# ScalarE puts the residual into PSUM ahead of the down product, and six pairs of row tiles go in seven products

## Chip, cores and metric

One core of a Trainium2 chip runs the whole layer in one launch. The metric is the device time of one execution in microseconds. The engines are TensorE (PE in the profile, its weight loads PEld), VectorE (DVE), ScalarE (ACT), GpSimd (POOL) and SyncE (SP, whose queue issues all loads and stores of the stage studied here).

## What is computed

A decoder layer on x of 256 tokens by 2048: a normalised input goes through one combined projection into gated linear attention and a sparse attention, both are joined by an output projection onto the residual, and a SwiGLU follows. The change is in the last two lines:

```python
h = x + jnp.concatenate([gla_out, nsa_out], axis=-1) @ w_out
m = rms_norm(h, ffn_norm_g)
return h + (jax.nn.silu(m @ w_gate) * (m @ w_up)) @ w_down
```

w_gate and w_up are 2048 x 5632, w_down is 5632 x 2048, all float32.

## The kernel before

**Precision.** Each float32 operand is split into a high and a low part (`in_parts`, lines 563 to 565: ScalarE copies the high part, VectorE subtracts to get the low one). A product is three matmuls: high x high, high x low weights, low x high.

**The feed-forward stage** walks over the 5632 columns in 11 blocks of 512 (`FB`, `NFB`). For each block f it runs `gate_up(f)`, and then, from the second block on, `down(f - 1)`: so the down product of a block comes after the gate and up products of the next, and the last down product stands alone at the end (lines 1075 to 1082).

**gate_up** (949 to 1026). The 16 row tiles of 128 are taken as 8 pairs. A pair's weights (two tiles of gate, two of up, 512 columns each) come in by two DMAs (`load4`, three buffers "fraw"). Gate and up, both token tiles (256 tokens are two tiles of 128) and both row tiles make a 2 x 2 x 2 product: eight products of 128x128 by 128x512, each of three matmuls. Some pairs (`PAIRS7`: 0, 2, 4, 5, 6; in the first block `FIRST7`: 0, 2, 4) are done in seven products instead, by combinations of the operands as in Strassen's scheme. On the side of the activations the combinations are made once (`pair_forms`, called from `turn_h` during the output projection); on the side of the weights they are made anew for each pair and block: VectorE adds (lines 983 to 985: one TT of 1024 elements, two of 512), and the four results are split as well. So a pair in eight costs one split of 2048 elements per partition, a pair in seven one of 1536 and two of 1024, and three TTs. Split weights lie in four buffers "ftwo" (`two_parts`); a pair in seven takes two of them, one with the plain weights (used by products 1, 2, 3: nine matmuls) and one with the combinations (products 5, 7, 6, 4: twelve). `ORDER0` and `ORDER` give the order of the pairs.

**Banks.** PSUM has eight banks of 128x512 float32. The products are added up in up to eight of them, numbered 1 to 8 in the code: 1, 5, 6, 7 belong to the sevens alone, 8 to the eights alone, 2, 3, 4 to both. `bank()` hands out the next of a pool of eight, in turn. After the last seven of a block (`last7`) banks 1, 5, 6, 7 are combined: ScalarE copies bank 1 to q1 (1008), VectorE makes u, q5u, q7u, q57u (1009 to 1012). At the end of the block these are added to banks 2, 3, 4, 8, and gate and up are put together with a Silu (1020 to 1025).

**turn_act** (1030 to 1039) is a generator that is fed in between the matmuls: it transposes the block's activations on TensorE, four transposes for each token tile, into a bank, and splits them into `hi` and `lo`. It runs near the end of the next block's gate_up (`urgent`); for the last block it is fed in during the down product before.

**down** (1041 to 1057) goes over the four column quarters n of the output: one load and split of w_down, 24 matmuls for both token tiles, then VectorE adds the two banks to the residual `h_sb[n]` in SBUF (line 1055); in the last call the result is stored by SP (1057), in halves of 256 columns.

**Order of the work.** The program is written as straight Python; a scheduler then fixes the order of the instructions on each engine, and each engine works its list through in order. Semaphores for data and for buffers are set by the framework.

Of the kernel before, what the change touches and what calls it, by code (L numbers as in the profile page):

```python
# [22 lines left out]
NFB = DFF // FB  # L23
# [13 lines left out]
def kernel(  # L37
# [4 lines left out]
    nc = tc.nc  # L42
    act, mm = nc.scalar.activation, nc.tensor.matmul
# [35 lines left out]
    urgent, later = [], []  # L79
# [11 lines left out]
    def drain(queue):  # L91
        while queue:
            for _ in queue.pop(0):
                pass

    def drive(mains, pace):

        credit = 0.0
        for m in mains:
            for units in m:  # L100
                credit += units
                while credit >= pace:
                    side()
                    credit -= pace

    last = {}
# [60 lines left out]
    for c in range(2):  # L167
        k = slice(2 * c, 2 * c + 2)
# [80 lines left out]
        rsqrt_(out, ms)  # L249


    def chunk(banks, xh, xl, ws, first_, end, parts=((0, 512),), t_first=False):

        order = [(k, t) for k in range(4) for t in range(NT)]
        if t_first:
            order.sort(key=lambda kt: kt[1])
        for k, t in order:
            wh, wl = ws[k]
            for i, (a, m) in enumerate(((xh, wh), (xh, wl), (xl, wh))):
                for (off, w), bk in zip(parts, banks):  # L260
                    last["mm"] = mm(  # L261
                        bk[t], a[:, k, t * P:(t + 1) * P], m[:, off:off + w],
                        start=(first_ and k == 0 and i == 0), stop=(end and k == 3 and i == 2))
                yield 2

    n_h, n_l = [], []
# [595 lines left out]

    PAIRS7, FIRST7 = (0, 2, 4, 5, 6), (0, 2, 4)


    OLD = (1, 3)
    ORDER0, ORDER = OLD + (0, 5, 2, 4, 6, 7), (0, 1, 2, 4, 3, 5, 6, 7)
    forms = {}  # L870
    turned = set()

# [67 lines left out]
    def parts_of(src):  # L940

        if not fw:
            return split(src, 4, 512)
        n = src.shape[1]
        hi, lo = two_parts()
        in_parts(hi[:, :n], lo[:, :n], src)
        return [(hi[:, k], lo[:, k]) for k in range(n)]

    def gate_up(fb, aTs, before):

        hi, lo = g4([4, S], F32R), g4([4, S], F32R)
        aTs.append((hi, lo))
        banks = {}

        def product(q, a, w, k):

            if q not in banks:
                banks[q] = bank()
                new = True
            else:  # L960
                new = False
            for i, (x, m) in enumerate(((a[0], w[k][0]), (a[0], w[k][1]), (a[1], w[k][0]))):
                todo[q] -= 1
                mm(banks[q], x, m, start=new and i == 0, stop=todo[q] == 0)  # L964

        def tokens(k, t):
            assert k in turned
            return tuple(x[k // 4][:, k % 4, t * P:(t + 1) * P] for x in (hT_h, hT_l))

        order, sevens = (ORDER0, FIRST7) if fb == 0 else (ORDER, PAIRS7)  # L970
        last7 = max(sevens, key=order.index)
        todo = dict.fromkeys((1, 5, 6, 7), 3 * len(sevens))
        todo.update(dict.fromkeys((2, 3, 4), 3 * len(sevens) + 6 * (8 - len(sevens))))
        todo[8] = 6 * (8 - len(sevens))
        for at, pair in enumerate(order):
            if fb == 0 and at == len(OLD):
                ffn_pools()
            a, b = 2 * pair, 2 * pair + 1
            r = load4([(m[0], a, 2, fb * FB) for m in (w_gate, w_up)])
            if pair in sevens:  # L980
                w = parts_of(r[:, 0:3])
                s1, s2 = g4([2, 512]), g4([2, 512])
                TT(s1, r[:, 1:3], r[:, 3:4].to_broadcast([P, 2, 512]), ALU.add)  # L983
                TT(s2[:, 0], s1[:, 1], r[:, 1], ALU.add)  # L984
                TT(s2[:, 1], s2[:, 0], r[:, 0], ALU.add)  # L985
                f = [tuple(forms[pair][:, i, j] for i in range(2)) for j in range(4)]
                product(1, tokens(b, 0), w, 1)
                yield 2
                product(2, tokens(a, 0), w, 0)
                yield 2  # L990
                product(3, f[3], w, 2)
                yield 2
                hi_, lo_ = two_parts()
                in_parts(hi_[:, 0:2], lo_[:, 0:2], s1)
                in_parts(hi_[:, 2:4], lo_[:, 2:4], s2)
                w = [(hi_[:, k], lo_[:, k]) for k in range(4)]
                for q, x, k in ((5, f[0], 0), (7, f[2], 1), (6, f[1], 2), (4, tokens(a, 1), 3)):
                    product(q, x, w, k)
                    yield 2
            else:  # L1000
                w = parts_of(r)
                for q, t, m in ((2, 0, 0), (3, 0, 1), (4, 1, 0), (8, 1, 1)):
                    for j in range(2):
                        product(q, tokens(a + j, t), w, 2 * m + j)
                        yield 2
            if pair == last7:
                q1, u, q5u, q7u, q57u = (g2([512]) for _ in range(5))
                act(q1, banks[1], AF.Copy)
                TT(u, banks[6], q1, ALU.add)
                TT(q5u, banks[5], u, ALU.subtract)  # L1010
                TT(q7u, banks[7], u, ALU.add)
                TT(q57u, banks[5], q7u, ALU.subtract)
                if before is not None:
                    urgent.append(before)
        if fb == 0:
            drain(urgent)
            rms(rf, ssh)
            TT(rf, rf, hback, ALU.mult)
        gs = []
        for t, (g, gq, u_, uq) in enumerate(((q1, 2, q5u, 3), (q7u, 4, q57u, 8))):  # L1020
            TT(g, banks[gq], g, ALU.add)
            act(g, g, AF.Silu, scale=rf[:, t:t + 1])
# [3 lines left out]
        turns[fb] = turn_act(gs, hi, lo)  # L1026

    turns = {}

    def turn_act(gs, hi, lo):  # L1030
        for t in range(NT):
            ts = slice(t * P, (t + 1) * P)
            p = bank()
            for j in range(4):
                transpose(p[:, j * P:(j + 1) * P], gs[t][:, j * P:(j + 1) * P])
                if j % 2:
                    yield
            pv = p.rearrange("p (j s) -> p j s", j=4)
            in_parts(hi[:, :, ts], lo[:, :, ts], pv)

    def down(f0, aTs, last):

        for m in range(2):
            banks = [[bank() for _ in range(NT)] for _ in range(2)]
            for f, (ah, al) in enumerate(aTs):
                end = f == len(aTs) - 1
                for i, n in enumerate((2 * m, 2 * m + 1)):
                    ws = parts_of(load4([(w_down[0], 4 * (f0 + f), 4, n * 512)]))
                    yield from chunk([banks[i]], ah, al, ws, f == 0, end, t_first=last and end)
                    if not end:  # L1050
                        continue
                    for t in range(NT):
                        for c in range(0, 512, 256 if last else 512):
                            cs = slice(c, c + (256 if last else 512))
                            TT(h_sb[n][:, t, cs], banks[i][t][:, cs], h_sb[n][:, t, cs], ALU.add)  # L1055
                            if last:
                                nc.sync.dma_start(out[t * P:(t + 1) * P, n * 512 + c:n * 512 + c + 256], h_sb[n][:, t, cs])


    drive([proj(C_LR, ev_go(0), ((0, 256), (256, 272)), first_chunk)], 2)  # L1060
# [11 lines left out]
    drain(later)  # L1072
    drive([w_out_half(1)], 6)

    acts = []
    for f in range(NFB):
        drive([gate_up(f, acts, turns.get(f - 1))], 2 if f == 0 else 3)
        if f == NFB - 1:
            urgent.append(turns[f])
        if f:  # L1080
            drive([down(f - 1, acts[f - 1:f], False)], 3)
    drive([down(NFB - 1, acts[NFB - 1:], True)], 3)


# [26 lines left out]
```

## Time and profile before

| | |
|---|---|
| Median of 3 runs | 1134.5 us (1133.68 to 1134.75) |
| The profiled execution | 1134.1 us |
| its span, first to last instruction | 1132.4 us |
| busy in the span: TensorE | 1120.4 us |
| VectorE | 965.9 us |
| ScalarE | 619.8 us |
| granted TensorE clock | 0.999 |

A row of a group gives: line, engine, operation, output<-input, shape, count, then busy time in us and mean ns of one, then the idle time of the engine just before such instructions and what ended it. A row of a timeline gives: start in us from the span's beginning, duration, engine, line, operation, shape, count, and in brackets the idle time ahead of it. A row of a chain gives start, length, what. A row of the windows gives the stretch, its length, then busy time and count for PE, PEld, DVE, ACT and POOL, the granted clock, the DMA share and GB/s. Consecutive instructions of one engine overlap by about 0.1 us, so the distance from start to start is what an instruction costs a busy engine.

### The profile page before, as it was taken

To read this page: it belongs to the slowest core of one execution; us is meant where nothing else is said; L and a number is where in the kernel's file an instruction comes from. 1 tells how busy PE (TensorE), PEld (TensorE's weight loads), DVE (VectorE), ACT (ScalarE), POOL (GpSimd) and SP (SyncE) were. 2 spreads that over 40 slices of the span, in tenths; PEclk is the share of its full clock that TensorE was granted. 3 is DMA by queue.
4 is the path that set the end of the run, shared out by engine and by line. 5 is a ranking of instruction groups with operands and counts; after the bars stand their busy time and mean duration, and the time that the engine had idled before them with its cause. 6 is when DMAs were issued, how large, how long until landed. Compare 5 with 4: busy or idle time off the path is not lost.

```text
span 1132.4 us, 14359 instructions
## 1 busy us (share of the span) xinstructions
PE 1120.4 (99%) x5515; PEld 927.1 (82%) x5515; DVE 965.9 (85%) x1205; ACT 619.8 (55%) x763; POOL 23.6 (2%) x53
## 2 busy tenths in 40 slices
PE   9999999999999999999999999999999999999998
PEld 8888889998777777788888888888888888888886
DVE  6547779987588678999999999999999999999993
ACT  7654466544466486664555546364555555464640
POOL 3000000100000000000000000000000000000000
PEclk9999999999999999999999999999999999999999
DMA  7655543445853354556665656555565556565652
GB/s 269 233 186 186 186 149 114 152 151 152 299 182 112 112 186 149 184 193 219 221 224 180 225 180 233 186 202 193 199 208 200 207 166 223 185 243 168 196 211 75
DMA packets 110446, 213.45 MB, mean 189 GB/s; under 512 B 5109, under 2 KB 8217, under 8 KB 110378
## 3 DMA queue, kind: packets, MB, share of 16 engines
q1 hardware_dynamic: 110378, 212.54, 56.1%
q8 instruction: 43, 0.70, 0.2%
q14 instruction: 25, 0.20, 0.1%
HBM read 210.42 MB, written 2.10 MB: 188 GB/s over the span
## 4 chain that ended last, share of the span: by engine, by line
PE 89%; issue 4%; DVE 4%; DMA 1%; POOL 0%; SPq 0%; ACT 0%; POOLq 0%; DVEq 0%
PE bank L261 45%; PE bank L964 37%; PE bank L193 3%; PE bank L817 1%; PE bank L759 1%; DVE ftwo L565 1%; DMA raw<-in_w_out_dram 1%; DVE lo L130 1%; DMA g<-in_x_dram 1%; PE bank L513 1%; DVE g L515 0%; DVE g L518 0%; DVE g L490 0%; PE bank L675 0%; DVE g L489 0%
## 5 line engine op out<-in xcount | busy, mean ns | idle before, releaser
L964 PE MATMUL bank<-ftwo,g 128*128 128x512 f32 x1905 | 444.9, 392 | 1.3 <-DVE ftwo L565 1.1
L964 PEld LDWEIGHTS bank<-ftwo,g 128*128 128x128 f32 x1905 | 354.0, 188 | 75.4 <-DVE ftwo L565 2.2
L261 PE MATMUL bank<-hi,g 128*128 128x512 f32 (+3 forms) x1152 | 326.3, 366 | 0.8 <-DVE g L615 0.6
L564 ACT ACTIVATE ftwo<-fraw 128x1536 fp32r<-128x1536 f32 (+1 forms) x130 | 226.3, 1741 | 141.5 <-PE bank L261 41.2
L565 DVE TENSOR_TENSOR ftwo<-fraw,ftwo 128x1536 fp32r<-128x1536 f32 (+1 forms) x130 | 267.2, 2067 | 13.8 <-ACT ftwo L564 13.8
L261 PE MATMUL bank<-ftwo,g 128*128 128x512 f32 x1056 | 241.9, 389 | 0.0
L261 PEld LDWEIGHTS bank<-ftwo,g 128*128 128x128 f32 x1056 | 198.0, 188 | 41.6 <-DVE g L565 0.4
L261 PEld LDWEIGHTS bank<-hi,g 128*128 128x128 f32 x1152 | 199.3, 189 | 30.9 <-issue 2.3
L130 DVE TENSOR_TENSOR lo<-raw,hi 128x1024 fp32r<-128x1024 f32 (+3 forms) x125 | 151.4, 1218 | 74.5 <-ACT hi L129 74.0
L564 ACT ACTIVATE ftwo<-g 128x1024 fp32r<-128x1024 f32 x106 | 110.5, 1058 | 158.9 <-DVE g L983 75.2
L261 PE MATMUL bank<-lo,g 128*128 128x512 f32 (+1 forms) x576 | 195.3, 365 | 0.5 <-DVE lo L130 0.5
L129 ACT ACTIVATE hi<-raw 128x1024 fp32r<-128x1024 f32 (+3 forms) x125 | 131.3, 1056 | 109.3 <-PE bank L261 77.5
L565 DVE TENSOR_TENSOR ftwo<-g,ftwo 128x1024 fp32r<-128x1024 f32 x106 | 127.2, 1217 | 8.2 <-ACT ftwo L564 8.2
L261 PEld LDWEIGHTS bank<-lo,g 128*128 128x128 f32 x576 | 102.6, 189 | 15.0 <-issue 0.9
L1055 DVE TENSOR_TENSOR g<-bank,g 128x512 f32<-128x512 f32 (+1 forms) x96 | 59.3, 642 | 15.6 <-PE bank L261 14.7
L983 DVE TENSOR_TENSOR g<-fraw 128x1024 f32<-128x1024 f32 x53 | 64.5, 1216 | 0.0
L564 ACT ACTIVATE g<-bank 128x512 fp32r<-128x512 f32 (+1 forms) x50 | 29.2, 587 | 21.8 <-PE bank L193 12.5
L193 PE MATMUL bank<-ident,g 128*128 128x128 f32 (+2 forms) x214 | 38.4, 278 | 2.4 <-DVE g L548 1.1
L565 DVE TENSOR_TENSOR g<-bank,g 128x512 fp32r<-128x512 f32 (+1 forms) x50 | 33.6, 681 | 7.7 <-ACT g L564 7.4
L193 PEld LDWEIGHTS bank<-ident,g 128*128 128x128 f32 (+2 forms) x214 | 27.5, 142 | 12.3 <-issue 2.3
L985 DVE TENSOR_TENSOR g<-g,fraw 128x512 f32<-128x512 f32 x53 | 36.3, 685 | 0.6
L984 DVE TENSOR_TENSOR g<-g,fraw 128x512 f32<-128x512 f32 x53 | 36.3, 685 | 0.5
(192 smaller groups left out, 639.3 us busy)
## 6 DMA issues: line engine op xcount, KB each, us to landing
fraw<-in_w_down_dram SPq DMA_DIRECT2D x44, 1024.0 KB, 5.1
fraw<-in_w_gate_dram SPq DMA_DIRECT2D x86, 512.0 KB, 3.8
fraw<-in_w_up_dram SPq DMA_DIRECT2D x86, 512.0 KB, 4.7
raw<-in_w_in_dram SPq DMA_DIRECT2D x36, 1024.0 KB, 5.1
raw<-in_w_out_dram SPq DMA_DIRECT2D x16, 1024.0 KB, 5.1
raw<-in_w_in_dram SPq DMA_DIRECT2D x4, 1072.0 KB
g<-in_x_dram SPq DMA_DIRECT2D x7, 512.0 KB, 9.8
raw<-in_w_in_dram SPq DMA_DIRECT2D x3, 1056.0 KB, 11.4
```

The source lines that it names most:

```text
L129: act(h[:, i:i + n], r[:, k + i:k + i + n], AF.Copy)
L130: TT(o[:, i:i + n], r[:, k + i:k + i + n], f32(h[:, i:i + n]), ALU.subtract)
L193: return nc.tensor.transpose(o, i, ident[:n, :n])
L261: last["mm"] = mm(bk[t], a[:, k, t * P:(t + 1) * P], m[:, off:off + w], start=(first_ and k == 0 and i == 0), stop=(end and k == 3 and i = ...
L513: mm(p[:, j * P:(j + 1) * P], u, w, start=True, stop=True)
L564: act(hi, ps, AF.Copy)
L565: TT(lo, ps, f32(hi), ALU.subtract)
L964: mm(banks[q], x, m, start=new and i == 0, stop=todo[q] == 0)
L983: TT(s1, r[:, 1:3], r[:, 3:4].to_broadcast([P, 2, 512]), ALU.add)
L984: TT(s2[:, 0], s1[:, 1], r[:, 1], ALU.add)
L985: TT(s2[:, 1], s2[:, 0], r[:, 0], ALU.add)
L1055: TT(h_sb[n][:, t, cs], banks[i][t][:, cs], h_sb[n][:, t, cs], ALU.add)
```

## The change

Four things, all in the feed-forward stage:

1. The sevens are pairs 0, 1, 2, 4, 5, 6, in the second block 0, 2, 4, 5, in the first as before. From the second block on the order is 0, 1, 3, 2, 4, 5, 6, 7.
2. The eight banks are allotted once and keep their numbers through all blocks. `turn_act` uses banks 1 and 5, the down product banks 6 and 7, 2 and 3, again 6 and 7, and 4 and 8 for its four quarters.
3. Before a quarter of the down product ScalarE copies the residual `h_sb[n]` into that quarter's two banks (`seed`), and the matmuls add to it without clearing. Afterwards ScalarE copies the banks back to `h_sb[n]`. VectorE's addition of line 1055 is gone.
4. `turn_act` waits two more steps and only then takes the buffers for its result. For the last block it is run after the down product of the block before, not during it.

```diff
-    PAIRS7, FIRST7 = (0, 2, 4, 5, 6), (0, 2, 4)
+    PAIRS7, FIRST7 = (0, 1, 2, 4, 5, 6), {0: (0, 2, 4), 1: (0,2,4,5)}
...
-    ORDER0, ORDER = OLD + (0, 5, 2, 4, 6, 7), (0, 1, 2, 4, 3, 5, 6, 7)
+    ORDER0, ORDER = OLD + (0, 5, 2, 4, 6, 7), (0, 1, 3, 2, 4, 5, 6, 7)
...
-                if before is not None:
-                    urgent.append(before)
+                if fb:
+                    urgent.append(turns[fb - 1])
+                    seed(0)
...
+    def turn_act(fb, gs):
+        for _ in range(2):
+            yield
+        hi, lo = acts[fb] = g4([4, S], F32R), g4([4, S], F32R)
...
-            p = bank()
+            p = banks[(1, 5)[t]]
...
-                            TT(h_sb[n][:, t, cs], banks[i][t][:, cs], h_sb[n][:, t, cs], ALU.add)
...
+    DOWN = ((6, 7), (2, 3), (6, 7), (4, 8))
+
+    def seed(n):
+        for t in range(NT):
+            nc.scalar.copy(banks[DOWN[n][t]], h_sb[n][:, t, :])
+
+    def down(f, last=False):
+        ah, al = acts.pop(f)
+        for n in range(4):
+            bs = [banks[q] for q in DOWN[n]]
+            ws = parts_of(load4([(w_down[0], 4 * f, 4, n * 512)]))
+            if n in (0, 2):
+                seed(n + 1)
+            yield from chunk([bs], ah, al, ws, False, True, t_first=last, onto=True)
+            for t in range(NT):
+                for c in range(0, 512, 256 if last else 512):
+                    cs = slice(c, c + (256 if last else 512))
+                    nc.scalar.copy(h_sb[n][:, t, cs], bs[t][:, cs])
+                    if last:
+                        nc.sync.dma_start(out[t * P:(t + 1) * P, n * 512 + c:n * 512 + c + 256], h_sb[n][:, t, cs])
+            if n == 0:
+                seed(2)
...
+        drive([gate_up(f)], 2 if f == 0 else 3)
         if f:
-            drive([down(f - 1, acts[f - 1:f], False)], 3)
-    drive([down(NFB - 1, acts[NFB - 1:], True)], 3)
+            drain(urgent)
+            drive([down(f - 1)], 3)
+    urgent.append(turns[NFB - 1])
+    drain(urgent)
+    seed(0)
+    drive([down(NFB - 1, True)], 3)
```

More of the change, by code (lines that the diff above doesn't have):

```diff
@@ L249, in rms, with chunk @@
         rsqrt_(out, ms)
-    def chunk(banks, xh, xl, ws, first_, end, parts=((0, 512),), t_first=False):
+    def chunk(banks, xh, xl, ws, first_, end, parts=((0, 512),), t_first=False, onto=False):
         order = [(k, t) for k in range(4) for t in range(NT)]
@@ L262, in chunk @@
                         bk[t], a[:, k, t * P:(t + 1) * P], m[:, off:off + w],
-                        start=(first_ and k == 0 and i == 0), stop=(end and k == 3 and i == 2))
+                        start=(first_ and k == 0 and i == 0), stop=(end and k == 3 and i == 2), skip_group_check=onto)
                 yield 2
@@ L947, in parts_of, with gate_up @@
         return [(hi[:, k], lo[:, k]) for k in range(n)]
[L949 to L953, printed above, removed]
+    banks = {}
+    def gate_up(fb):
         def product(q, a, w, k):
@@ L958, in product @@
                 banks[q] = bank()
[L959 to L962, printed above, removed]
+            for x, m in ((a[0], w[k][0]), (a[0], w[k][1]), (a[1], w[k][0])):
+                mm(banks[q], x, m, start=todo[q] == total[q], stop=todo[q] == 1)
                 todo[q] -= 1
-                mm(banks[q], x, m, start=new and i == 0, stop=todo[q] == 0)
         def tokens(k, t):
@@ L968, in tokens @@
             return tuple(x[k // 4][:, k % 4, t * P:(t + 1) * P] for x in (hT_h, hT_l))
-        order, sevens = (ORDER0, FIRST7) if fb == 0 else (ORDER, PAIRS7)
+        order, sevens = ORDER if fb else ORDER0, FIRST7.get(fb, PAIRS7)
         last7 = max(sevens, key=order.index)
@@ L974, in gate_up @@
         todo[8] = 6 * (8 - len(sevens))
+        total = dict(todo)
         for at, pair in enumerate(order):
@@ L1025, in gate_up @@
             gs.append(g)
-        turns[fb] = turn_act(gs, hi, lo)
-    turns = {}
-    def turn_act(gs, hi, lo):
+        turns[fb] = turn_act(fb, gs)
+    turns, acts = {}, {}
+    def turn_act(fb, gs):
+        for _ in range(2):
+            yield
+        hi, lo = acts[fb] = g4([4, S], F32R), g4([4, S], F32R)
         for t in range(NT):
             ts = slice(t * P, (t + 1) * P)
-            p = bank()
+            p = banks[(1, 5)[t]]
             for j in range(4):
@@ L1039, in turn_act @@
             in_parts(hi[:, :, ts], lo[:, :, ts], pv)
[L1041 to L1057, printed above, removed]
+    DOWN = ((6, 7), (2, 3), (6, 7), (4, 8))
[18 more added lines that the diff above has]
+                seed(2)
     drive([proj(C_LR, ev_go(0), ((0, 256), (256, 272)), first_chunk)], 2)
@@ L1073 @@
     drive([w_out_half(1)], 6)
-    acts = []
     for f in range(NFB):
-        drive([gate_up(f, acts, turns.get(f - 1))], 2 if f == 0 else 3)
-        if f == NFB - 1:
-            urgent.append(turns[f])
+        drive([gate_up(f)], 2 if f == 0 else 3)
         if f:
-            drive([down(f - 1, acts[f - 1:f], False)], 3)
-    drive([down(NFB - 1, acts[NFB - 1:], True)], 3)
+            drain(urgent)
[4 more added lines that the diff above has]
+    drive([down(NFB - 1, True)], 3)
 _INS = ['x', 'attn_norm_g', 'w_in', 'gla_conv_w', 'gla_gate_w2', 'gla_gate_b', 'gla_norm_g', 'nsa_q_norm_g',
```

## Prediction

> **What bounds the kernel now.** I read the page's first part, then its chain, then one block of the feed-forward stage.
>
> ```profile
> span 1132.4 us, 14359 instructions
> PE 1120.4 (99%) x5515; PEld 927.1 (82%) x5515; DVE 965.9 (85%) x1205; ACT 619.8 (55%) x763; POOL 23.6 (2%) x53
> PE 89%; issue 4%; DVE 4%; DMA 1%; POOL 0%; SPq 0%; ACT 0%; POOLq 0%; DVEq 0%
> L964 PE MATMUL bank<-ftwo,g 128*128 128x512 f32 x1905 | 444.9, 392 | 1.3 <-DVE ftwo L565 1.1
> 1015.04:1077.90 62.86, 62.86 (x283) 51.94 (x282) 59.98 (x58) 33.74 (x27) 0.00 (x0) 1.00 0.61 201
> ```
>
> TensorE carries the chain. In one whole block (the windows row) PE is busy for all of its 62.86 us, at granted clock 1.00; VectorE is busy 59.98, ScalarE 33.74. So in this stage time is the number of matmuls times the step of one, as long as nobody is late. The chain gives that step:
>
> ```profile
> 915.93 36.04 PE bank L964 x159
> 951.98 0.22 PE bank L193 x2
> 957.02 21.76 PE bank L261 x96
> ```
>
> 36.04 / 159 = 0.2267 us, and 21.76 / 96 the same; two transposes of an activation tile cost 0.22. A block has 177 + 96 matmuls and 8 transposes: 273 x 0.2267 + 0.9 = 62.8. The whole stage is explained by issue, and VectorE has 3 us to spare in each block.
>
> **What the change removes on PE.** A pair of row tiles in eight products is 24 matmuls (5.44 us), in seven 21 (4.76 us). Before, the first block has 3 sevens, each of the other ten 5; after: 3, then 4, then nine times 6. That is eight sevens more, 24 matmuls, 24 x 0.2267 = **5.44 us less**. Matmuls of the down product keep their count. Without new waits: 1134.1 - 5.4 = 1128.7.
>
> **What it adds elsewhere.** Steps from one instruction's start to the next one's on a busy engine:
>
> ```profile
> 887.84 2.28 DVE L565 TENSOR_TENSOR ftwo<-fraw,ftwo 128x2048 fp32r<-128x2048 f32 x1
> 890.04 0.68 DVE L1010 TENSOR_TENSOR f<-bank,f 128x512 f32<-128x512 f32 x1
> 890.64 0.68 DVE L1011 TENSOR_TENSOR f<-bank,f 128x512 f32<-128x512 f32 x1
> ...
> 908.28 1.22 DVE L565 TENSOR_TENSOR ftwo<-g,ftwo 128x1024 fp32r<-128x1024 f32 x1
> 909.42 1.22 DVE L983 TENSOR_TENSOR g<-fraw 128x1024 f32<-128x1024 f32 x1
> 910.55 1.28 DVE L1055 TENSOR_TENSOR g<-bank,g 128x512 f32<-128x512 f32 x2
> 911.75 1.21 DVE L565 TENSOR_TENSOR ftwo<-g,ftwo 128x1024 fp32r<-128x1024 f32 x1
> ...
> 923.23 1.75 DVE L565 TENSOR_TENSOR ftwo<-fraw,ftwo 128x1536 fp32r<-128x1536 f32 x1
> 924.90 0.68 DVE L984 TENSOR_TENSOR g<-g,fraw 128x512 f32<-128x512 f32 x1
> ```
>
> VectorE steps: 2.20 for 2048 elements, 1.67 for 1536, 1.13 for 1024, 0.60 for 512. A seven costs it 1.67 + 1.13 + 2 x 0.60 + 2 x 1.13 = 6.26, an eight 2.20: +4.1 us for each seven more. The residual additions of line 1055 leave: 8 x 0.60 = 4.8. Net -0.7 us in each of the nine blocks: no relief worth naming, and none needed.
>
> ScalarE gets 16 copies of 128x512 in each block, eight into PSUM, eight out. The rows next to them:
>
> ```profile
> L742 ACT COPY g<-bank 128x512 f32<-128x512 f32 x4 | 2.3, 586 | 3.2 <-DVE g L565 3.2
> L564 ACT ACTIVATE g<-g 128x512 fp32r<-128x512 f32 x13 | 8.1, 628 | 0.7 <-DVE g L880 0.3
> 891.68 0.57 ACT L564 ACTIVATE g<-bank 128x512 fp32r<-128x512 f32 x1
> 892.16 0.71 ACT L1022 ACTIVATE f<-f,rf 128x512 f32<-128x512 f32 x1
> ```
>
> PSUM to SBUF takes 0.59 (step 0.48). **No row shows ScalarE writing PSUM.** The nearest reads SBUF too and takes 0.63; I take that, step about 0.52. Ends: 0.48, if it is like the eviction, and 1.2, twice the row. So 16 x 0.5 = 8 us, and 33.7 becomes about 44 of 62.2: no bound by volume.
>
> [...]
>
> Moved and small parts together; their rows:
>
> ```profile
> 400.14 0.28 DVE L877 TENSOR_TENSOR g<-g 128x128 f32<-128x128 f32 x1
> ...
> 400.54 0.69 DVE L565 TENSOR_TENSOR g<-g,g 128x512 fp32r<-128x512 f32 x1
> ...
> 410.64 1.23 DVE L130 TENSOR_TENSOR lo<-raw,hi 128x1024 fp32r<-128x1024 f32 x1 [2.18 <-ACT hi L129]
> ...
> 1127.36 0.76 DVE L1055 TENSOR_TENSOR g<-bank,g 128x256 f32<-128x256 f32 x2 [1.96 <-PE bank L261]
> ```
>
> ```profile
> L464 ACT COPY g<-bank 128x256 f32<-128x256 f32 x8 | 2.6, 372 | 2.3 <-PE bank L193 2.3
> ```
>
> The combinations for pair 1 are computed once more, in the output projection: four TTs of 0.28 and a split of 0.69 on VectorE, 0.63 on ScalarE. There VectorE idles for 2.18 at a time, so 0; uncovered it would be about 2, once. SP issues the same loads in the same order, and its 16 stores at the end wait for ScalarE's copies of 0.37 instead of VectorE's additions of 0.38: 0. The second block gets easier for VectorE. What is left are the new orders of waiting, on ScalarE and in the fixed banks.
>
> From here on I use the order in which the changed program's instructions stand on each engine.
>
> **Wait 1: evictions stand in ScalarE's queue.** Behind the eviction of the last quarter of the down product, which waits for PE, stands the second half of pair 1's split. After the two copies it starts at about 0.7 us of the next block (time 0: PE's first matmul of a block); two ScalarE splits of 1024 and two of VectorE's, overlapped, end at 4.1; PE needs them at 4.76 + 2.04 = 6.8. Cost 0; it decides only if late by 2.7.
>
> **Wait 2: four sevens in a row** (pairs 2, 4, 5, 6). VectorE loses 6.26 - 4.76 = 1.5 us on each. But the split's four buffers hold it back harder than its volume: a split waits for the buffer of four tiles earlier.
>
> ```profile
> 915.77 36.20 PE L964 MATMUL bank<-ftwo,g 128*128 128x512 f32 x159
> 941.18 2.01 ACT L564 ACTIVATE ftwo<-g 128x1024 fp32r<-128x1024 f32 x2 [3.94 <-PE bank L964]
> 943.22 1.92 ACT L564 ACTIVATE ftwo<-fraw 128x2048 fp32r<-128x2048 f32 x1
> ```
>
> Here pair 3 ended 111 matmuls after 915.77, at 940.93, and ScalarE started 0.25 later. After the change PE's times are: pair 5's first half to 26.52, pair 6 from 29.24 to 34.00 (second half from 31.28), pair 7 to 39.44 with two pairs of transposes in it (0.45). Pair 7's split waits for pair 5's first half: ScalarE 26.77 to 28.69, VectorE from 28.72. In VectorE's order follow: pair 7 (2.20), the rest of pair 6's second half (1.14, done at 32.1; PE needs it at 32.9), down quarter 0 (2.20), u (0.60), quarter 1 (2.20), then q5u, q7u, the addition of bank 2, q57u (4 x 0.60). The last ends at 28.72 + 10.74 + 0.08 = 39.54.
>
> **Wait 3: the second activation tile.** That end now matters. Before, each transposed tile took a free bank; now tile 1 goes into bank 5, which q57u has to have read. So its four transposes, and the whole down product behind them, stand behind VectorE's 39.54. PE gets there at 39.9. Margin 0.3 us, on nine boundaries (the second block's two last pairs are both eights, there the margin is several us). After the transposes PE has four matmuls of tile 0, then needs tile 1's high part:
>
> ```profile
> 1086.75 0.63 PE L193 MATMUL bank<-ident,f 128*128 128x128 f32 x4
> 1087.13 40.18 PE L261 MATMUL bank<-ftwo,g 128*128 128x512 f32 x176
> 1087.41 0.60 ACT L564 ACTIVATE g<-bank 128x512 fp32r<-128x512 f32 x1 [1.59 <-PE bank L193]
> ```
>
> Next matmul 0.38 after the first transpose, ScalarE 0.66 after it, and 0.6 long: ready at 1.26 plus a hop of 0.05, wanted at 0.38 + 4 x 0.227 = 1.29. A wait of 0.0 to 0.2, I take 0.1. ScalarE must be free: its order there is seed of bank 7 (after q7u, 38.4), tile 0's split, a Silu, the seed of bank 2, tile 1's split: 38.4 + 0.52 + 0.5 + 0.62 + 0.52 = 40.56, and the transposes deliver at 39.9 + 0.66 = 40.56. No reserve. For both together (0.1, and a tenth for a VectorE that is sometimes late) I take 0.18 at each boundary: **+1.6**. Ends: 0 and about 0.6 each (0 to 5.4).
>
> **Wait 4: the last block.** Before, its transposes lay inside the previous down product:
>
> ```profile
> 1084.09 0.44 PE bank L193 x4
> 1086.85 0.53 PE bank L193 x4
> ```
>
> Now all eight stand at its end, and the last down product begins with them. ScalarE must first evict both last banks and reseed one (three copies, the first from 0.46 before PE's last issue): tile 0's split runs 1.17 to 1.76 after it, and PE, done with the transposes at 0.62, goes on at 1.8. Cost 1.8 against 0.97: **+0.9**. Ends 0.5 and 1.5.
>
> **Sum.** 1134.1 - 5.4 + 1.6 + 0.9 = **1131.2**, from the profiled execution's own time (span 1132.4, 1.7 around it); the median shown, 1134.5, is 0.4 above that, within which I don't correct.
>
> **Rivals.** *VectorE arrives late at bank 5.* For it: the margin of 0.3 comes from a sum of ten steps, and VectorE is 95% busy. Against: the start at 26.77 is tied to PE, so lateness doesn't grow from block to block. Late by 0.5 beyond the margin: nine times, 1131.2 + 4.5 - 0.9 = 1134.8: the saving is eaten.
>
> *ScalarE's write into PSUM is dear* (the slower side). Place: the two seeds ahead of tile 1's split. At 1.2 us each takes 0.6 more: 9 x 1.2 = 10.8, and 0.6 in the last block: 1142.6. It decides early: each 0.1 us per seed costs 1.9 us, so from 0.15 over my 0.52 on the change has lost its 2.9 us. For it: nothing in the trace shows this write; against: reading PSUM is no dearer than reading SBUF in the rows.
>
> *The row of four sevens starves PE* at pair 6's second half, where 0.8 us is left. Late by 1.5 there: 1131.2 + 9 x 0.7 = 1137.5.
>
> *The change doesn't add waits at all*: 1128.7 to 1129.5.
>
> **How the numbers follow.** Forecast 0.52 (its own range 1129.7 to 1133.0); no waits 0.08; late at bank 5 0.24 (1133 to 1136.5); dear seed 0.10 (1137 to 1143); starving 0.06 (1136 to 1140). About 0.2%, 2.3 us, is what a measurement of this kernel can tell from no change: below 1132.2 is faster, above 1136.8 slower. Faster: 0.42 of the forecast and the 0.08, 0.50. Same: the other 0.10 and the late bank, 0.34. Slower: dear seed and starving, 0.16. The range 1129.0 to 1136.5 leaves out half of the no-wait case and the slower ones, about 0.2.
>
> **What would show it.** In the windows of a block: 62.2 + 0.2 us; PE's matmuls of gate and up 1929 instead of 1953. In PE's waits: small ones on ScalarE's activation split at the start of a down product, one of about 1.2 us before the last. ScalarE busy near 44 per block, the copies at 0.6. A wait of PE's transposes for VectorE's q57u of over 0.3 per block, or copies into PSUM over 0.7, would prove me wrong; so would waits in the middle of the sevens.

## The result, and the profile after

The changed kernel takes **1130.46 us** (median of 6 runs, 1128.57 to 1132.2) against 1134.53 of the kernel before (6 runs, 1133.68 to 1136.78): ratio 0.9963, 95% interval 0.9948 to 0.9977. It is 4.1 us faster; 2.9 were forecast.

The page of the changed kernel, first part, chain, and the group of the gate and up matmuls:

```profile
span 1130.5 us, 14457 instructions
PE 1117.2 (99%) x5491; PEld 923.5 (82%) x5491; DVE 943.5 (83%) x1154; ACT 724.8 (64%) x964; POOL 23.6 (2%) x53
...
PE 88%; issue 4%; DVE 4%; DMA 2%; ACT 1%; SPq 0%; POOL 0%; POOLq 0%; ACTq 0%; DVEq 0%
...
L959 PE MATMUL bank<-ftwo,g 128*128 128x512 f32 x1881 | 435.2, 391 | 1.9 <-DVE ftwo L566 1.6
```

24 matmuls are gone (1905 to 1881 in this group), VectorE has 22 us less, ScalarE 105 more. One whole block in the windows, then the new copies (L1049 is the seed, L1062 the eviction):

```profile
644.81:706.99 62.18, 62.18 (x279) 51.33 (x279) 58.95 (x55) 43.47 (x46) 0.00 (x0) 1.00 0.61 202
```

```profile
L1062 ACT COPY g<-bank 128x512 f32<-128x512 f32 (+1 forms) x96 | 52.1, 552 | 78.3 <-PE bank L262 75.2
L1049 ACT COPY bank<-g 128x512 f32<-128x512 f32 x88 | 50.6, 592 | 10.9 <-DVE f L1006 6.8
```

This block went from 62.86 to 62.18, which is the 0.68 of one seven more and nothing else; the other whole blocks of the chain take 62.19 to 62.24, and one 62.41. A seed takes 0.592 us.

The profiled execution took 1132.2 us, the longest of the six runs. The reason lies far ahead of the change and has to be known before two traces are compared: the granted clock between 20 and 60 us, in the windows of the changed kernel (first fence) and of the kernel before (second).

```profile
20.00:60.00 40.00, 40.00 (x225) 34.09 (x224) 22.60 (x33) 25.43 (x38) 1.62 (x2) 0.96 0.58 194
```

```profile
20.00:60.00 40.00, 40.00 (x230) 34.17 (x229) 23.46 (x34) 27.07 (x39) 1.62 (x2) 1.00 0.62 204
```

The lower clock takes 1.7 us (last section), and the mark used below comes 2.15 us later than before. So I compare the traces from a mark behind it: the first group of 17 matmuls in the third pair of the first block, at 442.88 before and at 445.03 after.

```profile
442.88 4.23 PE L964 MATMUL bank<-ftwo,g 128*128 128x512 f32 x17 [0.25 <-ACT ftwo L564]
```

```profile
445.03 4.27 PE L959 MATMUL bank<-ftwo,g 128*128 128x512 f32 x17 [0.24 <-ACT ftwo L565]
```

From there the chains of before (first) and after (second) give three stretches: (a) to the end of the first down product, (b) to the start of the last but one down product, (c) to PE's last matmul.

```profile
516.78 21.76 PE bank L261 x96
538.54 36.04 PE bank L964 x159
...
1082.72 1.37 PE bank L261 x6
...
1087.38 39.95 PE bank L261 x176
```

```profile
520.24 21.76 PE bank L262 x96
542.00 36.72 PE bank L959 x162
...
1080.29 21.17 PE bank L262 x93
...
1103.76 22.09 PE bank L262 x96
```

| stretch (us) | before | after | difference | of it matmuls |
|---|---|---|---|---|
| (a) mark to 538.54 / 542.00 | 95.66 | 96.97 | +1.31 | +0.68 |
| (b) to 1082.72 / 1080.29 | 544.18 | 538.29 | -5.89 | -6.12 |
| (c) to 1127.33 / 1125.85 | 44.61 | 45.56 | +0.95 | 0 |
| sum | 684.45 | 680.82 | -3.63 | -5.44 |

5.44 us of matmuls are saved, 1.8 come back: 0.63 in the second block, 0.23 at all the boundaries, 0.95 in the last block. The 0.23 is a net figure: one down product of the changed kernel takes 22.01 (at 582.40) and one of the kernel before 22.04 (at 831.04), where the others take 21.82 to 21.84 and 21.76.

### The profile page after: what moved, and what is told of

It reads as the page before. It is cut to its first block, busy times and chain, and to the rows that moved or that the text cites. A ratio compares the mean times of both kernels' runs of the same rounds, so it can differ in the third digit from the quotient of the medians.

```text
span 1130.5 us, 14457 instructions
## 1 busy us (share of the span) xinstructions
PE 1117.2 (99%) x5491; PEld 923.5 (82%) x5491; DVE 943.5 (83%) x1154; ACT 724.8 (64%) x964; POOL 23.6 (2%) x53
## 4 chain that ended last, share of the span: by engine, by line
PE 88%; issue 4%; DVE 4%; DMA 2%; ACT 1%; SPq 0%; POOL 0%; POOLq 0%; ACTq 0%; DVEq 0%
PE bank L262 46%; PE bank L959 36%; PE bank L193 3%; DVE ftwo L566 1%; PE bank L818 1%; PE bank L760 1%; PE bank L514 1%; DMA raw<-in_w_out_dram 1%; DMA g<-in_x_dram 1%; DVE lo L130 1%; DVE g L516 0%; DVE g L519 0%; DMA fraw<-in_w_up_dram 0%; ACT hi L129 0%; PE bank L676 0%
## 5 line engine op out<-in xcount | busy, mean ns | idle before, releaser
L959 PE MATMUL bank<-ftwo,g 128*128 128x512 f32 x1881 | 435.2, 391 | 1.9 <-DVE ftwo L566 1.6
L566 DVE TENSOR_TENSOR ftwo<-fraw,ftwo 128x1536 fp32r<-128x1536 f32 (+1 forms) x130 | 262.4, 2035 | 24.6 <-ACT ftwo L565 24.3
L565 ACT ACTIVATE ftwo<-fraw 128x1536 fp32r<-128x1536 f32 (+1 forms) x130 | 222.8, 1714 | 44.1 <-PE bank L959 15.7
L262 PE MATMUL bank<-ftwo,g 128*128 128x512 f32 x1056 | 242.9, 391 | 0.8 <-ACT g L565 0.8
L565 ACT ACTIVATE ftwo<-g 128x1024 fp32r<-128x1024 f32 x122 | 125.9, 1056 | 82.6 <-PE bank L959 51.1
L566 DVE TENSOR_TENSOR ftwo<-g,ftwo 128x1024 fp32r<-128x1024 f32 x122 | 146.4, 1219 | 6.6 <-ACT ftwo L565 6.6
L1062 ACT COPY g<-bank 128x512 f32<-128x512 f32 (+1 forms) x96 | 52.1, 552 | 78.3 <-PE bank L262 75.2
L980 DVE TENSOR_TENSOR g<-fraw 128x1024 f32<-128x1024 f32 x61 | 74.4, 1220 | 4.6 <-DMA fraw<-in_w_up_dram 4.5
L1049 ACT COPY bank<-g 128x512 f32<-128x512 f32 x88 | 50.6, 592 | 10.9 <-DVE f L1006 6.8
L981 DVE TENSOR_TENSOR g<-g,fraw 128x512 f32<-128x512 f32 x61 | 41.9, 687 | 0.7
L982 DVE TENSOR_TENSOR g<-g,fraw 128x512 f32<-128x512 f32 x61 | 41.8, 685 | 0.3
```

Of the source, the lines that this page charges most:

```text
L262: last["mm"] = mm(bk[t], a[:, k, t * P:(t + 1) * P], m[:, off:off + w], start=(first_ and k == 0 and i == 0), stop=(end and k == 3 and i = ...
L565: act(hi, ps, AF.Copy)
L566: TT(lo, ps, f32(hi), ALU.subtract)
L959: mm(banks[q], x, m, start=todo[q] == total[q], stop=todo[q] == 1)
L1049: nc.scalar.copy(banks[DOWN[n][t]], h_sb[n][:, t, :])
L1062: nc.scalar.copy(h_sb[n][:, t, cs], bs[t][:, cs])
```

## Experiments

Theory from here on: the seed wins nothing by itself; it frees VectorE, and that is what makes the sixth seven payable. Rival: one of the two parts alone brings the gain. Then come the three waits that gave 1.8 us back. Each run is given by its median and ratio to the kernel before, and by the stretches of its one profiled execution from the same mark, which the early clock doesn't touch. The ratio is to runs of the kernel before on the same chip in the same job. Where waits break the down product into pieces, only the sum of the stretches is given.

| kernel | us | ratio, 95% interval | (a) | (b) | (c) | sum |
|---|---|---|---|---|---|---|
| before | 1134.53 | 1 | 95.66 | 544.18 | 44.61 | 684.45 |
| after | 1130.46 | 0.9963 (0.9948 to 0.9977) | 96.97 | 538.29 | 45.56 | 680.82 |
| seed alone | 1137.69 | 1.0025 (1.0015 to 1.0036) | 96.50 | 544.53 | 45.55 | 686.58 |
| sevens alone | 1147.86 | 1.0119 (1.0103 to 1.0134) | | | | 697.45 |
| tile 0 first | 1130.25 | 0.9961 (0.9949 to 0.9974) | 96.87 | 537.86 | 45.54 | 680.27 |
| seeds late | 1128.89 | 0.9950 (0.9938 to 0.9963) | 96.27 | 538.20 | 45.13 | 679.60 |
| last turn early | 1130.04 | 0.9955 (0.9941 to 0.9968) | 96.91 | 538.22 | 44.57 | 679.70 |
| second block, five | 1130.81 | 0.9967 (0.9955 to 0.9979) | 96.34 | 538.83 | 45.54 | 680.71 |
| second block, old | 1131.36 | 0.9969 (0.9959 to 0.9980) | 96.85 | 538.13 | 45.52 | 680.50 |
| old order | 1134.66 | 0.9996 (0.9986 to 1.0005) | 96.14 | 543.32 | 45.66 | 685.12 |
| seven sevens | 1144.06 | 1.0078 (1.0064 to 1.0091) | | | | 693.93 |
| three edits | 1128.70 | 0.9940 (0.9926 to 0.9954) | 96.33 | 537.86 | 44.52 | 678.71 |
| after, again | 1130.94 | 0.9964 (0.9952 to 0.9977) | 96.63 | 538.23 | 45.52 | 680.38 |

The changed kernel has two profiled executions, the rows "after" and "after, again". They differ by 0.34 us in (a), 0.06 in (b) and 0.04 in (c). So a difference of some tenths says something in (b) and (c), but not in (a).

### The seed alone

```diff
-    PAIRS7, FIRST7 = (0, 1, 2, 4, 5, 6), {0: (0, 2, 4), 1: (0,2,4,5)}
+    PAIRS7, FIRST7 = (0, 2, 4, 5, 6), {0: (0, 2, 4)}
...
-    ORDER0, ORDER = OLD + (0, 5, 2, 4, 6, 7), (0, 1, 3, 2, 4, 5, 6, 7)
+    ORDER0, ORDER = OLD + (0, 5, 2, 4, 6, 7), (0, 1, 2, 4, 3, 5, 6, 7)
```

> The new banks, the seeds and the later transposes alone, with the five sevens and the order of the kernel before (1953 matmuls of gate and up). My theory: the seed buys no time by itself, because VectorE was not late before; what is left are the new waits, about 0.1 us at each of ten boundaries and 0.9 us at the last block, so 1.9 us slower than before, about 1136.4; VectorE falls from 60 to about 55 us in a block of 62.9. Rival: VectorE's relief by itself takes hidden waits away, then the time is below that of the kernel before.

The stretches are 2.1 us longer than before (0.84 + 0.35 + 0.94), near the theory's 1.9, but only the last block's 0.94 lies where the theory put it. The boundaries of (b) cost 0.35 in place of 0.9, and the 0.84 of (a) stands against one boundary's 0.1, so the agreement of the sums is in part luck. The median is 3.2 over that of the kernel before, part of it the early clock (0.91 between 20 and 60 us in its profiled execution). One block in its windows:

```profile
647.05:709.98 62.93, 62.93 (x283) 51.91 (x282) 55.45 (x50) 41.84 (x44) 0.00 (x0) 1.00 0.60 200
```

VectorE is down from 59.98 to 55.45 and the block is no shorter than the 62.86 of before: VectorE was not late, and freeing it gained the kernel nothing.

### The sevens alone

```diff
-            nc.scalar.copy(banks[DOWN[n][t]], h_sb[n][:, t, :])
+            pass
...
-            yield from chunk([bs], ah, al, ws, False, True, t_first=last, onto=True)
+            yield from chunk([bs], ah, al, ws, True, True, t_first=last)
...
-                    nc.scalar.copy(h_sb[n][:, t, cs], bs[t][:, cs])
+                    TT(h_sb[n][:, t, cs], bs[t][:, cs], h_sb[n][:, t, cs], ALU.add)
```

> The changed kernel with its sevens, order and fixed banks, but the residual is added by VectorE again, and ScalarE neither seeds nor evicts. My theory: VectorE gets 8 additions of 0.60 us on top of its 58.9 in a block, 63.7 against 62.1 of TensorE, so VectorE sets the block and the nine blocks with six sevens cost about 1.6 us more each: 1130.5 + 14 = 1144.5, and PE waits within the sevens. Rival: VectorE's busy time overlaps enough, or the buffers carry it over, and the time stays at 1130 to 1132; then the sevens alone bring the gain and the seed is no part of it.

16.6 us more than the changed kernel in the stretches (14 expected). One block in its windows, and the waits of its matmuls on the page:

```profile
1030.07:1094.68 64.61, 63.51 (x279) 51.07 (x279) 63.57 (x63) 34.80 (x30) 0.00 (x0) 1.00 0.59 196
```

```profile
L959 PE MATMUL bank<-ftwo,g 128*128 128x512 f32 x1881 | 438.6, 392 | 9.4 <-DVE ftwo L566 8.7
```

VectorE is busy 63.57 in the block of 64.61, more than the 62.18 of the changed kernel: it sets the time, and PE waits for its splits. The rival falls: neither part gains alone, both together do. The matmuls are saved by the sevens; the seed only pays VectorE's bill for them. This run keeps the fixed banks and the later transposes; six sevens with the banks of the kernel before were not run.

### Seven sevens

```diff
-    PAIRS7, FIRST7 = (0, 1, 2, 4, 5, 6), {0: (0, 2, 4), 1: (0,2,4,5)}
+    PAIRS7, FIRST7 = (0, 1, 2, 3, 4, 5, 6), {0: (0, 2, 4), 1: (0,2,4,5)}
```

> The changed kernel with a seventh seven (pair 3) in each of the nine last blocks. By PE's count 3 matmuls less in a block: 61.5 us instead of 62.2, 6.1 us in all, 1124.4. My theory: VectorE, 58.9 us in a block of 62.2 now, gets 4.1 more, 63.0, and so sets the block; in the kernel without the seed it was busy for 63.7 and the block took 64.1. So 63.4 or more for a block, nine times 1.2 over now: 1141, and PE waits for VectorE's splits. Rival: VectorE's lateness is carried by the buffers over the down product, then the blocks are 61.5 to 62 and the time is 1124 to 1129.

1144.06, slower than expected by 3. One block in its windows:

```profile
967.25:1030.97 63.72, 62.52 (x276) 50.63 (x276) 62.59 (x60) 44.82 (x48) 0.00 (x0) 1.00 0.58 196
```

VectorE has 62.59 of work where PE's matmuls need 61.5. As the program stands six are the limit, also with the seed. But PE's matmuls do not wait where the theory said, at the weight splits. Their waits and those of its transposes between 542 and 1080 us (in all, how many, the longest):

```profile
PE bank L193 <- DVE f L1009: 6.0, 8, 0.9
PE bank L262 <- ACT bank L1049: 4.2, 8, 1.0
```

VectorE's lateness reaches PE at the end of a block, through q57u (L1009) and bank 5 and through the seeds behind it: the place of the prediction's first rival.

### The boundary: tile 0 first, and seeds behind the split

```diff
-            yield from chunk([bs], ah, al, ws, False, True, t_first=last, onto=True)
+            yield from chunk([bs], ah, al, ws, False, True, t_first=last or n == 0, onto=True)
```

> The changed kernel, but in the first quarter of each down product the twelve matmuls of token tile 0 come ahead of those of tile 1, so the split of tile 1's activations is wanted 8 matmuls (1.8 us) later. My theory: what is left at a boundary is PE's wait of about 0.08 us for that split, so nine boundaries give 0.7 us, 1129.8; the first down product of a block lasts 21.76 instead of 21.84. Rival: the extra of a block over its matmuls lies elsewhere (transposes, VectorE at bank 5); then nothing changes.

```diff
-            ws = parts_of(load4([(w_down[0], 4 * f, 4, n * 512)]))
+            with behind(acts["split"] if n == 3 else None):
+                ws = parts_of(load4([(w_down[0], 4 * f, 4, n * 512)]))
             if n in (0, 2):
-                seed(n + 1)
+                with behind(acts["split"]):
+                    seed(n + 1)
```

Here `behind` only sets the order on ScalarE, and `acts["split"]` is its split of tile 1 (the lines that record it are not shown).

> The changed kernel, but on ScalarE the seeds of quarters 1 and 3 and one weight split are queued behind the split of tile 1's activations. My theory: this takes the same 0.08 us off each of nine boundaries (0.7 us), and in the last block the seed that stands between the two evictions and the activation split, 0.55 us: together 1.2 us, 1129.2. Rival: the seeds moved back are late for their own quarter (they are wanted 5.4 us after the boundary), then the down product gets a wait between its first and second quarter and the time rises.

Both expectations were too high at the boundary. With tile 0 first, (b) is 0.4 us shorter in nine boundaries, not 0.7; with the seeds late it is 0.1 shorter, no more than the changed kernel's own two executions differ by. The same down product in two chains, first the changed kernel, then the one with tile 0 first:

```profile
955.86 21.84 PE bank L262 x96
```

```profile
954.04 21.81 PE bank L262 x96
```

That is 0.03 a boundary; half of the 0.4 is the changed kernel's 22.01 at 582.40, which its second execution lacks. The wait for tile 1's split is there, on PE's weight loads, in the changed kernel between 539 and 1085 us:

```profile
PEld bank L262 <- ACT g L565: 1.9, 9, 0.4
```

With tile 0 first the weight loads have no such wait there; with the seeds late it is 1.7 us in nine waits. So a seed ahead of the split is not what makes it late, and of the 0.2 us that a weight load waits the chain gets back only 0.03. What is left over the 96 matmuls (21.76) I can't put down to a wait. The median with tile 0 first, 0.2 lower, says no more.

What the late seeds did gain is (c), 0.43 of the 0.55 expected. Their (a) is 0.70 shorter too, which is not shown to be this edit's doing (see "The second block"). In the chain of the changed kernel, a seed stands between the two evictions and the split on which the last down product waits:

```profile
1101.49 0.59 ACT g L1062
1102.10 0.59 ACT bank L1049
1102.69 0.52 ACT g L1062
1103.21 0.51 ACT g L565
1103.76 22.09 PE bank L262 x96
```

In the chain of the kernel with late seeds it is gone from there:

```profile
1100.88 0.59 ACT g L1065
1101.47 0.51 ACT g L565
```

### The last block's tiles turned early

```diff
         if f:
             drain(urgent)
+            if f == NFB - 1:
+                urgent.append(turns[f])
             drive([down(f - 1)], 3)
-    urgent.append(turns[NFB - 1])
```

> The changed kernel, but the last block's activation tiles are transposed and split during the down product before, as in the kernel before. My theory: the new end of that down product (transposes, then three copies of ScalarE ahead of the split) is what costs 0.9 us in the last block; undone, the last two down products lose it: 1129.6, and from the start of the last but one down product to PE's end it is 44.6 us instead of 45.6. Rival: the two transposed tiles and ScalarE's splits now cut into the evictions and seeds of that down product, and the wait only moves there: no change.

(c) is 44.57, that of the kernel before. So the 0.95 was this one move, shown by undoing it. The median moved by 0.4 only, less than the runs of one kernel differ by.

### The second block

Five sevens, in the new order:

```diff
-    PAIRS7, FIRST7 = (0, 1, 2, 4, 5, 6), {0: (0, 2, 4), 1: (0,2,4,5)}
+    PAIRS7, FIRST7 = (0, 1, 2, 4, 5, 6), {0: (0, 2, 4), 1: (0, 2, 4, 5, 6)}
```

> The changed kernel with five sevens in the second block (pair 6 too) instead of four. Theory 1, by count: 3 matmuls less, 0.68 us, 1129.8. Theory 2: the second block has no down product in which VectorE can catch up (a seven costs it 6.26 against 4.76 of PE); its 42 us for four sevens already exceed PE's 41.2, so a fifth costs 1.5 more and wins 0.7: 0.8 slower, 1131.3, with PE waiting for VectorE's splits late in the second block. Both are read from the second block alone, 70.6 us from its first matmuls to the first down product now.

Five sevens, in the order of before (this edit beside the one above):

```diff
-        order, sevens = ORDER if fb else ORDER0, FIRST7.get(fb, PAIRS7)
+        order, sevens = (ORDER0, (0, 1, 2, 4, 3, 5, 6, 7), ORDER)[min(fb, 2)], FIRST7.get(fb, PAIRS7)
```

> The changed kernel with the second block as in the kernel before: five sevens, order 0, 1, 2, 4, 3, 5, 6, 7. In the kernel before this stretch took 69.2 us, in the changed one 70.6, of which 0.68 are the missing seven. Theory: the rest, 0.65, is the place of the two eights (two in a row, whose loads come late, then three sevens with VectorE behind); with the old second block it goes away with the count: 1.3 us less, 1129.2. Rival: it belongs to the fixed banks and the later transposes; then only the 0.68 comes back, 1129.8, or less if VectorE is late for the fifth seven.

Neither theory held as it stood. The fifth seven shortened (a) by 0.63 (by 0.29 against the changed kernel's second execution), but (b) grew by 0.54: the next block takes 62.87 in place of 62.41, so it is paid one block later. With the old order (a) stayed at 96.85, and the sum lies between the two executions of the changed kernel. The medians of both are within 0.9 of the changed kernel. So four sevens in the second block are not a loss.

Nor is the place of the two eights shown to cost anything. First, the old order does not take the loss away: with the very pairs and order of the kernel before, (a) is 1.19 longer than there in this run, and 0.84 in the one with the seed alone. Second, PE's wait ahead of this block's splits, 0.80 in the kernel before, is 1.03 or 1.04 in every changed kernel, in either order; here before and seed alone (old order):

```profile
479.75 29.30 PE L964 MATMUL bank<-ftwo,g 128*128 128x512 f32 x127 [0.80 <-DVE ftwo L565]
```

```profile
483.48 29.60 PE L959 MATMUL bank<-ftwo,g 128*128 128x512 f32 x128 [1.03 <-DVE ftwo L566]
```

Third, the rest changes from execution to execution. From 470 us to its end this block is the same program in the changed kernel and in the one with late seeds: VectorE, ScalarE and SP take the same instructions in the same order. PE's waits in it, in the changed kernel and then with the seeds late:

```profile
481.88 27.17 PE L959 MATMUL bank<-ftwo,g 128*128 128x512 f32 x118 [1.04 <-DVE ftwo L566]
509.39 1.66 PE L959 MATMUL bank<-ftwo,g 128*128 128x512 f32 x6 [0.33 <-DVE ftwo L566]
```

```profile
481.38 28.47 PE L959 MATMUL bank<-ftwo,g 128*128 128x512 f32 x124 [1.04 <-DVE ftwo L566]
```

The second wait is gone, and (a) is 96.27: no longer than 95.66 plus the missing seven's 0.68, in the new order. ScalarE's timeline shows where the two part, some 7.6 and 6.0 us after the first of these rows starts:

```profile
489.50 1.49 ACT L565 ACTIVATE ftwo<-fraw 128x1536 fp32r<-128x1536 f32 x1 [2.02 <-DMA fraw<-in_w_up_dram]
```

```profile
487.42 1.50 ACT L565 ACTIVATE ftwo<-fraw 128x1536 fp32r<-128x1536 f32 x1 [0.44 <-PE bank L959]
```

In the changed kernel a weight split waits for its load, with the late seeds the load is there in time, though SP issued it at the same distance from that row (3.8 us for its second half). The load is late in the kernels with tile 0 first and with the last turn early too (96.87, 96.91), and in time in the changed kernel's second execution (96.63). What makes it land late stays open.

### The old order

```diff
-    ORDER0, ORDER = OLD + (0, 5, 2, 4, 6, 7), (0, 1, 3, 2, 4, 5, 6, 7)
+    ORDER0, ORDER = OLD + (0, 5, 2, 4, 6, 7), (0, 1, 2, 4, 3, 5, 6, 7)
```

> The changed kernel with its six sevens in the order of the kernel before (0, 1, 2, 4, 3, 5, 6, 7): the four sevens in a row stand at the start of a block, right behind the down product, and two before the last pair. My theory: a block is as long as its matmuls in either order, because VectorE comes out of the down product with all buffers filled: 1130.5, blocks of 62.2. Rival: four sevens in a row cost VectorE 6 us more than PE wherever they stand; behind the last eight of the block before there is less reserve, PE waits for splits in the first pairs, and the block gets longer by 0.5 to 1.5 us, 1135 to 1144.

My theory fell. All of the gain is gone (0.9996), by the stretch (b): 5 us over nine blocks, though not for the reason the rival gave: PE has no wait in the first pairs. Two blocks make up 3.3 of it, with 64.08 and 63.64; the other whole blocks take 62.43 to 62.72. PE's timeline at the dearest boundary shows where it stands, and ScalarE's below it what stands in the queue:

```profile
827.71 0.96 PE L959 MATMUL bank<-ftwo,g 128*128 128x512 f32 x3
829.50 0.44 PE L193 MATMUL bank<-ident,f 128*128 128x128 f32 x2 [0.83 <-DVE f L1009]
```

```profile
827.22 1.92 ACT L565 ACTIVATE ftwo<-fraw 128x2048 fp32r<-128x2048 f32 x1 [1.74 <-DMA fraw<-in_w_down_dram]
829.04 0.58 ACT L1049 COPY bank<-g 128x512 f32<-128x512 f32 x1
829.55 0.72 ACT L1020 ACTIVATE f<-f,rf 128x512 f32<-128x512 f32 x1
830.18 0.58 ACT L565 ACTIVATE g<-bank 128x512 fp32r<-128x512 f32 x1
```

Tile 1's transposes wait 0.83 for q57u (L1009), and on ScalarE a weight split that waited 1.74 for its load stands ahead of a seed, a Silu and the activation split. This is the "late at bank 5" of my first rival, together with ScalarE's queue, in another order of pairs. In the changed kernel the same place has room, by VectorE's timeline and then PE's:

```profile
829.77 0.68 DVE L1009 TENSOR_TENSOR f<-bank,f 128x512 f32<-128x512 f32 x1
```

```profile
830.83 0.60 PE L193 MATMUL bank<-ident,f 128*128 128x128 f32 x4
```

q57u is through at 830.45, the transposes start at 830.83. So the new order is a third part of the change, without which it is worth nothing. What in the order makes the load late (a buffer of "fraw" freed later by VectorE is my reading of the chain) was not tried by itself.

(a) was 0.83 shorter with it than in the changed kernel's profiled execution. That the old order is the better one for the second block's four sevens is not shown by it: the late seeds, in the new order, have an (a) as short.

### Three edits together

The old order in the second block alone (four sevens kept), the last tiles turned early (as above), tile 0 first:

```diff
-        order, sevens = ORDER if fb else ORDER0, FIRST7.get(fb, PAIRS7)
+        order, sevens = (ORDER0, (0, 1, 2, 4, 3, 5, 6, 7), ORDER)[min(fb, 2)], FIRST7.get(fb, PAIRS7)
...
-            yield from chunk([bs], ah, al, ws, False, True, t_first=last, onto=True)
+            yield from chunk([bs], ah, al, ws, False, True, t_first=last or n == 0, onto=True)
```

> The changed kernel with three edits: the second block's pairs in the order 0, 1, 2, 4, 3, 5, 6, 7 with its four sevens kept, the last activation tiles turned during the down product before, and tile 0's matmuls first in each first quarter. Measured from the matmuls ahead of the second block to PE's last, the parts gave 0.83, 1.12 and 0.27 us by themselves. My theory: they lie at different places and add up, 2.2 us: 1128.3, against 1130.5 of the changed kernel. Rival: the second block's gain is no order but which way ScalarE's queue fell in that program, and does not come again; then 1129.1.

1128.70 against 1130.94 of the changed kernel, which ran beside it unchanged:

> The changed kernel once more, beside the two others on the same chip: 1130.5, with 1128.5 to 1132.2 by the granted clock between 20 and 60 us, which differs from execution to execution in every kernel.

The sum of the stretches is 678.71 (678.6 follows from the parts); that of the changed kernel 680.82 and, again, 680.38. (b) is 537.86, just that of tile 0 first, and (c) 44.52, that of the last turn early: these two gains repeat and add up, some 1.4 us. (a) is 96.33, the 95.66 of before plus the one missing seven's 0.68, but as the late seeds reach 96.27 in the new order, the order's share in it is not shown. This version beats both kernels: 0.6% under the kernel before, 2.2 us under the changed one. By its median the kernel with the late seeds (1128.89) is as good; by the stretches it is 0.9 longer.

## Why the prediction was right, and where it was not

**Bound and count: right.** 24 matmuls less, 5.44 us; blocks of gate and up stand in the chain as `36.72 ... x162`, 0.2267 each, unbroken.

**VectorE and ScalarE: right.** VectorE went from 59.98 to 58.95 (1.0 less, forecast 0.7), ScalarE to 43.47 (44). "No relief worth naming, and none needed" was half of the truth: without the relief the sixth seven would have cost 16.6 us, as the kernel without the seed showed. The prediction had that sum in its hands (59.98 + 4.1 is over 62.2) and did not draw it.

**The seed's price: right.** Taken as 0.63 long, step 0.52; it is 0.592, step 0.51 (the changed kernel's ScalarE timeline in the last but one down product):

```profile
1083.24 0.59 ACT L1049 COPY bank<-g 128x512 f32<-128x512 f32 x1
1083.75 0.59 ACT L1062 COPY g<-bank 128x512 f32<-128x512 f32 x1
```

The dear seed falls: a write into PSUM took 592 ns, against the 628 of the nearest row that stays in SBUF (which also writes another type, fp32r) and the 587 of the eviction, a read from PSUM into SBUF.

**Wait 1, wait 2: right, with a condition.** No wait of PE's matmuls is listed within the nine blocks. But that the four in a row cost nothing holds for their place, as the old order showed; the prediction never asked what the order of the pairs was worth.

**Wait 3: the mis-sized term.** Forecast 0.18 a boundary, 1.6 in all; measured 0.23 in all, about 0.03 a boundary. The first tenth, tile 1's split, is there on PE's weight loads (0.2 a boundary), but hardly reaches its matmuls: over matmuls and transposes alone a block now has 62.18 against 270 x 0.2267 + 0.9 = 62.11, and the kernel before has the same surplus, 62.86 against 62.79. And the tenth for a late VectorE did not come: the margin at bank 5 was 0.38 us at the boundary shown, where I had worked out 0.3.

**Wait 4: right.** 0.9 forecast (its own 1.8 against 0.97 makes 0.83), 0.95 measured, and gone when undone. PE's wait there for the activation split is 0.75, not 1.2.

**What was missed.** "The second block gets easier for VectorE", at a cost of nothing: PE waited there for VectorE's splits, 1.04 and then 0.33, where before there was only the first wait, of 0.80 (the rows stand under "The second block"). The 0.24 more at the first wait comes in every changed kernel whatever the order of the pairs; the 0.33 came in an execution in which a load landed at least 1.5 us later than in others of the same program. Together with small rests this cost 0.63 in the profiled execution and 0.29 in the second one. Which part of the change brings the 0.24, the fixed banks, the seeds or the later transposes, stays open.

So the sum of -5.4 + 1.6 + 0.9 became -5.44 + 0.23 + 0.95 + 0.63 = -3.63 in the stretches. That it came so near the forecast -2.9 is in part luck: a wait sized 1.4 too high stood against one of 0.63 that was taken as nothing. Another 0.4 lies behind PE's last matmul (1132.4 - 1127.33 = 5.07 before, 1130.5 - 1125.85 = 4.65 after); the kernel with the sevens alone, where VectorE still adds, has 4.63 there, so it is not the eviction's. What it is stays open.

## What to carry over

Before an engine's work is called slack, add up what the other half of the change puts on it: here each half alone made the kernel slower, one by 0.25%, one by 1.2%, and only both, in the right order of pairs, made it faster. Where a second engine is as near the bound as VectorE is here, 58.95 of 62.18, the order of the work can decide as much as its amount, so try the order by itself. Compare two traces from a mark behind anything that differs by chance, and before a few tenths in one stretch are put down to a cause, profile the same kernel twice.

## Not expected of the hardware

The clock at the start. In the changed kernel's profiled execution the granted clock fell to 0.50 between 47 and 51 us, in the windows:

```profile
47.00:48.00 1.00, 1.00 (x4) 0.76 (x4) 1.00 (x1) 0.98 (x2) 0.00 (x0) 0.64 1.07 410
48.00:49.00 1.00, 1.00 (x4) 0.81 (x3) 0.22 (x1) 0.99 (x2) 0.00 (x0) 0.50 0.20 76
49.00:50.00 1.00, 1.00 (x4) 0.71 (x4) 0.00 (x0) 0.88 (x1) 0.00 (x0) 0.50 0.00 0
50.00:51.00 1.00, 1.00 (x4) 0.84 (x3) 0.00 (x0) 0.00 (x0) 0.00 (x0) 0.66 0.00 0
```

The lost clock adds up to 1.7 us (0.36 + 0.50 + 0.50 + 0.34). The kernel with the seed alone shows 0.91 over the 40 us, 3.6 us lost, about twice as much; the kernel before shows none in its profiled execution. PE is busy in all these rows. Just ahead stand small matmuls of 17 rows (44 to 47 us), but five of the thirteen traces, with the same matmuls, keep 1.00 over the 40 us. What lowers the clock was not shown. The lost 1.7 us is only a part of why runs of one kernel differ: four of the changed kernel's six runs, all at a mean clock of 1.000, still lie between 1128.57 and 1131.49. The cause of that stays open.
